# An encoder trunk on one core: three quarters of three turned inputs go through DRAM in 32x32 blocks

## The chip, the cores and the metric

The kernel runs on one core of a Trainium2 chip. The time is that of the whole program on the device, in microseconds (us); for the kernel before, the median of three runs is 2045.74 us (2043.22 to 2048.05).

A core has five engines that run their own instruction queues in order: TensorE (PE, with weight loads listed as PEld), VectorE (DVE), ScalarE (ACT), GpSimd (POOL) and SyncE (SP), which here issues most of the transfers. Semaphores tie the queues together.

## The reference

An encoder of two layers over 256 tokens of 2048 features, batch 1, float32. In each layer a token mixer of 12 heads and 4 cross-attention heads into 256 memory tokens work side by side on one input projection; their outputs are concatenated and go through one output projection; a squared-ReLU MLP of width 8192 follows. Layer 0 mixes by neighbourhood attention, layer 1 by grouped-query attention.

```python
m = rms_norm(mem, mem_norm)
h = x
for i in range(2):
    n = rms_norm(h, attn_norm[i])
    z = n @ w_in[i]                      # a_w_in in layer 0, b_w_in in layer 1
    ...                                  # mixer heads and memory heads
    h = h + concatenate([mix, cross]) @ w_o[i]
    n = rms_norm(h, mlp_norm[i])
    h = h + square(relu(n @ w_up[i])) @ w_down[i]
return rms_norm(h, final_norm)
```

where `rms_norm(x, g) = x * rsqrt(mean(x*x) + EPS) * g`. Since relu is homogeneous, `square(relu(c*x)) = c*c*square(relu(x))` for a positive factor c per token: an MLP may be fed with an input that is scaled by another positive factor than the exact one, if its output is corrected by the square of their ratio. The kernel uses this.

## The kernel before

**Precision.** Every float32 operand of a large product is split into a high part (rounded to the matmul's input type by ACT, `Copy`) and a low part (DVE, original minus high). A product is then three matmuls: high by high, low by high, high by low. So each weight chunk costs a load by SP, an ACT instruction and a DVE instruction (function `split`, lines 306 and 307) before PE uses it.

**Layout.** The running state `h` keeps tokens on partitions: 2 token tiles (`NT`) of 128, each 2048 features wide. A projection contracts over features, so its input must have features on partitions. It lies in a tile of one buffer, tag `wide` (`nT0`, `hT0`, `nT1`, `hT1` in turn): for each of 16 feature tiles k, 256 columns of the high part and 256 of the low part. Turning `h` into this form is what the change is about. In the kernel before `transposed` does it: for two feature tiles at a time, four PE transposes of 128x128 into one PSUM tile `pt_n` (line 324), then per feature tile `split_pair`: ACT multiplies by the gain and rounds (line 332), DVE computes the low part (line 333).

**Order of the work.** The program is a list of grains, run one after the other; a grain of a projection is 12 matmuls of 128x512 (or 24 of 128x256 in the up projection). `halves_of`, `up_grains`, `down_grains` and `plain_grains` make them. Loads and splits of a grain's weights are emitted some grains ahead (`ahead`, by default 8, 5 and 3 grains for its three stages; `SOON` 8, 5 and 4). After each grain `tick` counts one up and runs what `later(n, fn)` has put n ticks ahead. This gives every instruction its place in program order; a planner then simulates the engines and lets each engine take, at each simulated moment, the first instruction in program order that is ready. `past(fn)` adds an edge, so that what `fn` emits on ACT and DVE stands behind a given split in the queue of its engine.

**Buffers.** Weight halves of a projection have four buffers (`hi`, `lo` of pool `ring`); where a stage of the MLP is near, the halves `uh` and `ul` have two (pool `side`). Pool `side` also has the tags `U` (2 raw chunks), `b` (2, of 3 x 512 columns: pair chunks of the down projection) and `T` (2, of 4 x 512 columns: scaled blocks of `h`, later the fourth columns `t` of the pair chunks and raw chunks of the plain stage).

**Output projection and MLP input.** `add_o` computes the output projection in four blocks of 512 columns. Blocks 0 and 1 run interleaved (block 0 ends with its 14th grain, block 1 with its 16th), then block 2 (24th) and block 3 (32nd). `o_done` follows each block's last grain: it adds the block to `h` (line 687) and sums its squares (line 629). At block 2 `guard` estimates the mean square from three blocks (`GUARD`), POOL raises it to the power -1/2 (line 653), and `scaled` and `transposed` bring the three blocks to PE; block 3 is scaled beforehand in `begun`, gets its product added (line 704), and is turned at last. `inv` computes the ratio that corrects the MLP's output, from the exact mean square and the estimate `near`.

**From layer 0 to layer 1.** The last part of the down projection is the plain stage: four blocks of 512 columns, four grains each. `down_done` adds each block to `h` (line 880), sums its squares, and one tick later turns that block of `h` unscaled into `nT1`, on PE, for layer 1's input projection; that projection's results are scaled by `rstd` afterwards. Layer 1's projection starts with three chunks of the memory queries (`b_qm_done`), grains with `uh` and `ul`; chunk c reads the feature tiles of block c.

**A way through DRAM that is there already.** Layer 0's attention turns its 12 score tiles not on PE but by `turned`: DVE transposes every 32x32 block within its 32 partitions (line 393), and `moved` brings the blocks to their places: four SP transfers, one for each group of 32 partitions, write to a DRAM tile (line 358), and one POOL transfer reads it back (line 359).

Of the kernel before, what the change touches and what calls it, by code (L numbers as in the profile page):

```python
# [17 lines left out]
P = 128  # L18
# [18 lines left out]
PARTS = 8  # L37
PK = DFF // PARTS // P
STEPS = PK // 2
GUARD = 3  # L40

MOVING_AT = 160

# [35 lines left out]
def encoder_kernel(ctx: ExitStack, tc: tile.TileContext, t: dict, out: bass.AP):  # L79
# [70 lines left out]
    def halves_of(w):  # L150

        tiles = {}

        def load():
            tiles["raw"] = loaded(w.src, "U")

        def prep_early(hf):
            tiles[hf] = half_of_side(tiles["raw"], hf, MOVING_AT)

        def prep(hf):  # L160
            if hf == 0:
                tiles["raw"] = at.ring.tile([P, CH], F32, tag="raw", bufs=3, name="raw")
                nc.sync.dma_start(tiles["raw"], w.src)
            tiles[hf] = new_half(w.kind)
            split(*tiles[hf], tiles["raw"][:, hf * HALF : (hf + 1) * HALF])

        def run(hf):
            if hf == 0:
                w.start(w)
            hi, lo = tiles.pop(hf)  # L170
            if w.kind == "S":
                s_products(w, hf * (KT // 2), KT // 2, hi, lo)
            else:
                for i in range(NT):
                    m_products(w, w.first + 2 * hf, 2, i, hi, lo, w.begins and hf == 0, w.last and hf == 1)

        def after():
# [17 lines left out]
    def later(n, fn, *args):  # L195
        pending.append((state["tick"] + n, fn, args))
# [362 lines left out]
    def x_stats():  # L559
        ss = small.tile([P, NT], F32, tag="ss0", name="x_ss")  # L560
        for i in range(NT):
            for b in range(4):
                sq = at.work.tile([P, 512], F32, tag="b_y2", name="sq")
                nc.scalar.activation(sq, h[:, i, b * 512 : (b + 1) * 512], AF.Square, accum_out=ssq[0][:, i, b : b + 1])
        nc.vector.tensor_reduce(ss, ssq[0], axis=AX.X, op=ALU.add)
        box["x_col"] = keep.tile([P, NT], F32, name="x_col")
        nc.vector.tensor_copy(box["x_col"], rstd_of(ss, D, "x"))
        box["x_row"] = at.work.tile([P, SEQ], F32, tag="x_row", bufs=1, name="x_row")
        along_free(box["x_col"], box["x_row"])

# [69 lines left out]
    def past(fn, ins=None):  # L640

        a, v = ins or box["ready"]
        with tc.issue_after(a.ins), tc.issue_after(v.ins):
            fn()

    def o_done(layer, nb):
        which = 2 * layer

        def guard():

            box["near"] = mean_square(which, GUARD, "near")
            box["scale"] = keep.tile([P, NT], F32, tag="scale", name="scale")
            nc.gpsimd.tensor_tensor(box["scale"], box["near"], mhalf[:, :NT], op=ALU.pow)
            box["hT"] = wide(f"hT{layer}")

        def begun():

            y = at.side.tile([P, NT, 512], F32, tag="T", bufs=2, name="h_s")
            for i in range(NT):
                nc.scalar.activation(y[:, i, :], h[:, i, D - 512 :], AF.Copy, scale=box["scale"][:, i : i + 1])  # L660
            box["begun"] = y

        def scaled(b):
            y = at.side.tile([P, NT, 512], F32, tag="T", bufs=2, name="h_s")
            for i in range(NT):
                nc.scalar.activation(y[:, i, :], h[:, i, b * 512 : (b + 1) * 512], AF.Copy,
                                     scale=box["scale"][:, i : i + 1])
            transposed(box["hT"], lambda i, k: y[:, i, k % 4 * P : (k % 4 + 1) * P],
                       list(range(b * 4, b * 4 + 4)), (G_M0, G_M1)[layer])

        def inv():

# [7 lines left out]
        def f(w):  # L680
            if nb == 0:
                closed("work")
                at.side = opened("side", side="right")
            def add():
                for i in range(NT):
                    hs = h[:, i, nb * 512 : (nb + 1) * 512]
                    nc.vector.tensor_tensor(hs, w.ps[i], hs, op=ALU.add)

            def squares():
                for i in range(NT):  # L690
                    sum_squares(which, i, nb)

            if nb < 3:
                add()
                squares()
            if nb == GUARD - 1:
                later(1, guard)
                for b in range(GUARD):
                    later(2 + 2 * b, scaled, b)
                later(7, begun)  # L700
            if nb == 3:
                y = box["begun"]
                for i in range(NT):
                    nc.vector.scalar_tensor_tensor(y[:, i, :], w.ps[i], box["scale"][:, i : i + 1], y[:, i, :],
                                                   op0=ALU.mult, op1=ALU.add)
                box["ready"] = transposed(box["hT"], lambda i, k: y[:, i, k % 4 * P : (k % 4 + 1) * P],
                                          list(range(12, KT)), (G_M0, G_M1)[layer])
                later(4, past, add)
                later(6, past, squares)
                later(8, past, inv)  # L710
# [200 lines left out]
    def plain_grains(layer, nb):  # L911
# [9 lines left out]
        def prep(c, hf):  # L921
            if c == 0:
                own[c, hf] = half_of_side(own[0], hf, PLAIN_AT)
            else:
                own[c, hf] = tuple(at.mlp.tile([P, HALF], F32R, tag="bt"[hf] + x, name=f"{x}_p") for x in "hl")
                split(*own[c, hf], own[1][:, hf * HALF : (hf + 1) * HALF])

        PIECES = ((0, 0, 0, 2), (0, 1, 2, 2), (1, 0, 4, 2), (1, 1, 6, 2))

# [51 lines left out]
    def times_gf(nb):  # L981
        s = slice(nb * 512, (nb + 1) * 512)
        for i in range(NT):
            nc.vector.tensor_tensor(h[:, i, s], h[:, i, s], box["gf"][:, s], op=ALU.mult)

    def down_done(layer, nb):
        def f(w):
            for i in range(NT):
# [5 lines left out]
                return  # L994
            if nb == 0:
                box["nT"] = wide("nT1", 480)
            later(1, transposed, box["nT"], lambda i, k: h[:, i, k * P : (k + 1) * P],
                  list(range(nb * 4, nb * 4 + 4)), G_A1)
            if nb == 3:
                closed("mlp")  # L1000
                open_ring()

                def norm():
                    box["rstd"] = keep.tile([P, NT], F32, name="rstd1")
                    v = mean_square(1, 4, "full")
                    nc.gpsimd.tensor_tensor(box["rstd"], v, mhalf[:, :NT], op=ALU.pow)
                later(2, norm)
        return f

# [268 lines left out]
```

## Time and profile before

| | us |
|---|---|
| median of three runs | 2045.74 |
| lowest, highest | 2043.22, 2048.05 |
| the profiled execution | 2041.28 |
| its span, first to last instruction | 2039.5 |
| PE busy in it | 2018.9 |
| DVE busy | 1665.5 |
| ACT busy | 1241.9 |
| POOL busy | 125.3 |

The granted TensorE clock is full (mean 0.999). The busy time of PE is that of records that overlap: a matmul of 128x512 is recorded as about 390 ns, but one starts every 227 ns. So PE's own pace is read from starts, not from durations. The transfers move 440.16 MB, nearly all of it weights that SP loads.

### The profile page before, as it was taken

Reading aid. Unit: us, or ns where it says so; the run is one execution under the profiler, and the core shown is the slowest. Engines: PE = TensorE matmul, PEld = TensorE weight load, DVE = VectorE, ACT = ScalarE, POOL = GpSimd, SP = SyncE. Lnnn points to the kernel's source line nnn. Section 1 sums busy time; section 2 is a strip of 40 time slices with the busy share of each in tenths; the row PEclk is TensorE's granted clock in tenths of the full one; section 3 lists DMA queues with packets and bytes.
Section 4 is the critical chain, followed back from the end, with each engine's and each line's share of the span. In section 5 each row is a group of like instructions: output and inputs, shape, how many; then the busy total and the mean of one; then the engine's idle time right before and its main releaser. Section 6 shows DMA issues by size and latency. Waiting matters only on the chain.

```text
span 2039.5 us, 32742 instructions
## 1 busy us (share of the span) xinstructions
PE 2018.9 (99%) x13044; PEld 1827.2 (90%) x13044; DVE 1665.5 (82%) x2049; ACT 1241.9 (61%) x1628; POOL 125.3 (6%) x156
## 2 busy tenths in 40 slices
PE   8999999999999999999999999999999999999998
PEld 7899999889999999999988888889999999999986
DVE  6767677558989999989997667657999999999896
ACT  6655455456666666666656557556666666666654
POOL 0000000000000000010000001000000000000000
PEclk9999999999999999999999999999999999999999
DMA  7756666727778787777765454537777787777773
GB/s 281 276 200 202 218 211 213 287 83 239 231 220 240 222 239 229 224 236 232 229 207 220 176 170 145 199 113 235 236 230 231 222 239 228 231 224 230 230 220 137
DMA packets 101306, 440.16 MB, mean 216 GB/s; under 512 B 11424, under 2 KB 19232, under 8 KB 68000
## 3 DMA queue, kind: packets, MB, share of 16 engines
q1 hardware_dynamic: 82800, 402.40, 58.4%
q0 software_dynamic: 17776, 34.61, 9.1%
q8 instruction: 102, 1.67, 0.3%
q10 hardware_dynamic: 576, 1.05, 0.1%
q14 instruction: 52, 0.43, 0.1%
HBM read 401.32 MB, written 7.34 MB: 200 GB/s over the span
## 4 chain that ended last, share of the span: by engine, by line
PE 95%; DVE 2%; DMA 1%; issue 1%; ACT 1%; SPq 0%; POOLq 0%; POOL 0%; DVEq 0%; ACTq 0%
PE ps_u L742 11%; PE ps_u L740 11%; PE ps_u L741 11%; PE p L859 9%; PE p L858 9%; PE p L857 8%; PE ps_m L214 8%; PE ps_m L217 8%; PE ps_m L218 8%; PE ps_s L226 3%; PE ps_s L228 3%; PE ps_s L227 3%; DVE ul L307 1%; DMA raw<-in_w_km 1%; PE pt_n L324 1%
## 5 line engine op out<-in xcount | busy, mean ns | idle before, releaser
L742 PE MATMUL ps_u<-hT,ul 128*128 128x256 f32 x2048 | 567.1, 277 | 2.3 <-DVE ul L307 2.3
L740 PE MATMUL ps_u<-hT,uh 128*128 128x256 f32 x2048 | 565.6, 276 | 0.1
L741 PE MATMUL ps_u<-hT,uh 128*128 128x256 f32 x2048 | 565.6, 276 | 0.0
L306 ACT ACTIVATE uh<-raw_U 128x1024 fp32r<-128x1024 f32 x278 | 294.6, 1060 | 306.6 <-PE ps_u L741 280.2
L740 PEld LDWEIGHTS ps_u<-hT,uh 128*128 128x128 f32 x2048 | 384.5, 188 | 5.7 <-ACT uh L306 0.5
L741 PEld LDWEIGHTS ps_u<-hT,uh 128*128 128x128 f32 x2048 | 384.3, 188 | 5.4
L742 PEld LDWEIGHTS ps_u<-hT,ul 128*128 128x128 f32 x2048 | 384.4, 188 | 4.5 <-DVE ul L307 3.5
L307 DVE TENSOR_TENSOR lo<-raw,hi 128x1024 fp32r<-128x1024 f32 (+1 forms) x224 | 266.1, 1194 | 148.8 <-ACT hi L306 147.4
L307 DVE TENSOR_TENSOR ul<-raw_U,uh 128x1024 fp32r<-128x1024 f32 x278 | 337.2, 1218 | 38.9 <-ACT uh L306 38.8
L306 ACT ACTIVATE hi<-raw 128x1024 fp32r<-128x1024 f32 (+1 forms) x224 | 231.5, 1039 | 205.4 <-PE ps_m L218 112.2
L306 ACT ACTIVATE th<-t 128x2048 fp32r<-128x2048 f32 x112 | 215.1, 1921 | 124.4 <-PE p L859 116.1
L307 DVE TENSOR_TENSOR tl<-t,th 128x2048 fp32r<-128x2048 f32 x112 | 256.1, 2287 | 29.9 <-ACT th L306 29.4
L307 DVE TENSOR_TENSOR bl<-b,bh 128x1536 fp32r<-128x1536 f32 x112 | 196.0, 1750 | 0.3
L858 PE MATMUL p<-tl,a_s 128*128 128x512 f32 x448 | 176.1, 393 | 0.3 <-DVE tl L307 0.3
L859 PE MATMUL p<-th,a_s 128*128 128x512 f32 x448 | 176.3, 394 | 0.0
L306 ACT ACTIVATE bh<-b 128x1536 fp32r<-128x1536 f32 x112 | 166.2, 1484 | 7.7 <-PE p L859 1.3
L837 POOL DMA_DIRECT2D t<-b x112 | 96.4, 860 | 1157.1 <-DVE t L836 551.8
L857 PE MATMUL p<-th,a_s 128*128 128x512 f32 x448 | 163.6, 390 | 0.0
L859 PE MATMUL p<-bh,a_s 128*128 128x512 f32 x336 | 131.7, 392 | 0.0
L858 PE MATMUL p<-bl,a_s 128*128 128x512 f32 x336 | 131.0, 390 | 0.0
L228 PE MATMUL ps_s<-nT,lo 128*128 128x256 f32 x448 | 125.4, 280 | 0.0
L226 PE MATMUL ps_s<-nT,hi 128*128 128x256 f32 x448 | 125.2, 279 | 0.0
(237 smaller groups left out, 3770.2 us busy)
## 6 DMA issues: line engine op xcount, KB each, us to landing
raw_U<-in_w_up SPq DMA_DIRECT2D x128, 1024.0 KB, 6.4
b<-in_w_pair SPq DMA_DIRECT2D x112, 768.0 KB, 4.5
raw<-in_w_o SPq DMA_DIRECT2D x32, 1024.0 KB, 5.0
t<-in_w_pair SPq DMA_DIRECT2D x112, 256.0 KB, 3.4
t<-b POOLq DMA_DIRECT2D x112, 256.0 KB, 6.7
raw<-in_w_b SPq DMA_DIRECT2D x21, 1024.0 KB, 5.0
raw<-in_w_av SPq DMA_DIRECT2D x12, 1024.0 KB, 5.0
raw<-in_w_aq SPq DMA_DIRECT2D x12, 1024.0 KB, 4.9
```

The lines of the kernel that those rows point to most:

```text
L214: first = nc.tensor.matmul(w.ps[i], ah, hi[:, s], start=st, stop=False)
L217: nc.tensor.matmul(w.ps[i], ah, lo[:, s], start=False, stop=False)
L226: nc.tensor.matmul(ps, hi[:, s], acts[:, k, :SEQ], start=k == 0, stop=False)
L228: nc.tensor.matmul(ps, lo[:, s], acts[:, k, :SEQ], start=False, stop=k == KT - 1)
L306: first = nc.scalar.activation(dst_hi, src, AF.Copy)
L307: return first, nc.vector.tensor_tensor(dst_lo, src, dst_hi.bitcast(F32), op=ALU.subtract)
L740: nc.tensor.matmul(ps, hi[:, s], acts[:, k, :SEQ], start=k == 0, stop=False)
L741: nc.tensor.matmul(ps, hi[:, s], acts[:, k, SEQ:], start=False, stop=False)
L742: nc.tensor.matmul(ps, lo[:, s], acts[:, k, :SEQ], start=False, stop=k == KT - 1)
L857: nc.tensor.matmul(ps, a[:, 0, ai, :], hi[:, s], start=begins, stop=False)
L858: nc.tensor.matmul(ps, a[:, 0, ai, :], lo[:, s], start=False, stop=False)
L859: nc.tensor.matmul(ps, a[:, 1, ai, :], hi[:, s], start=False, stop=ends)
```

## The change

1. **The MLP input's factor.** Both MLPs' inputs are no longer scaled by the inverse root mean square of three finished blocks of `h`, but by that of the input of the same layer, which is known since before the projection: `x_col` in layer 0, `rstd` in layer 1. `inv` uses the corresponding mean squares (`x_mean`, `mean`). `guard` and `GUARD` are gone. So a block can be scaled as soon as it has been added.
2. **Blocks 0 to 2 of both MLP inputs** are scaled right after their add (`turning`), turned in 32x32 blocks by DVE and moved through DRAM (`turned_rows`). Block, room and read-back share one tile of tag `T`. `landed` makes the high and the low part from the read-back 6, 6 and 5 ticks later (`LANDED`), behind the last split emitted by then. Block 3 is left as it was.
3. **Blocks 0 to 2 of the second layer's input** go the same way, unscaled, through two tiles of tag `b` (`turned_input`), with `landed` 6 ticks later. Block 3 stays on PE.

`landed` emits per feature tile one ACT instruction over 256 columns and two DVE instructions over 128. `box["splits"]` now also collects the splits of `halves_of` and `plain_grains`, which `landed_past` needs.

```diff
-GUARD = 3
+TURNED = 3
+
+LANDED = 6, 6, 5
...
         box["x_col"] = keep.tile([P, NT], F32, name="x_col")
-        nc.vector.tensor_copy(box["x_col"], rstd_of(ss, D, "x"))
+        box["x_mean"] = keep.tile([P, NT], F32, name="x_mean")
+        nc.vector.tensor_scalar(box["x_mean"], ss, 1.0 / D, EPS, op0=ALU.mult, op1=ALU.add)
+        nc.gpsimd.tensor_tensor(box["x_col"], box["x_mean"], mhalf[:, :NT], op=ALU.pow)
...
+    def turned_rows(src, room, back):
+
+        nc.vector.transpose(room.rearrange("p (b k i j) -> p i k b j", b=4, k=4, i=2),
+                            src.rearrange("p i (k b r) -> p i k b r", k=4, b=4))
+        back = back.rearrange("p (a f) -> p a f", a=4)
+        moved(back, room.rearrange("p (b f) -> p b f", b=4))
+        return back
+
+    def landed(dst, back, b, which):
+
+        src = back.rearrange("p a (k i j) -> p k i a j", k=4, i=2)
+        for k in range(4):
+            n, g = b * 4 + k, gain(which, b * 4 + k)
+            hi, lo = (dst[:, n, x * SEQ : (x + 1) * SEQ].rearrange("p (i a j) -> p i a j", i=2, a=4) for x in range(2))
+            nc.scalar.activation(hi, src[:, k], AF.Copy, scale=g)
+            for i in range(NT):
+                nc.vector.scalar_tensor_tensor(lo[:, i], src[:, k, i], g, hi[:, i].bitcast(F32),
+                                               op0=ALU.mult, op1=ALU.subtract)
+
+    def landed_past(*args):
+        past(lambda: landed(*args), box["splits"][-1])
...
-        def guard():
-
-            box["near"] = mean_square(which, GUARD, "near")
-            box["scale"] = keep.tile([P, NT], F32, tag="scale", name="scale")
-            nc.gpsimd.tensor_tensor(box["scale"], box["near"], mhalf[:, :NT], op=ALU.pow)
+        def factors():
+
+            box["scale"] = box[("x_col", "rstd")[layer]]
+            box["near"] = box[("x_mean", "mean")[layer]]
             box["hT"] = wide(f"hT{layer}")
...
+        def turning():
+
+            y = at.side.tile([P, 2, NT, 512], F32, tag="T", bufs=2, name="h_s")
+            scaled(y[:, 0], nb)
+            x, room = (y[:, n].rearrange("p a b -> p (a b)") for n in range(2))
+            back = turned_rows(y[:, 0], room, x)
+            later(LANDED[nb], landed_past, box["hT"], back, nb, (G_M0, G_M1)[layer])
...
             if nb < 3:
                 add()
+                turning()
                 squares()
-            if nb == GUARD - 1:
-                later(1, guard)
-                for b in range(GUARD):
-                    later(2 + 2 * b, scaled, b)
-                later(7, begun)
+            if nb == 2:
+                later(3, begun)
...
+    def turned_input(nb):
+
+        x, y = (at.side.tile([P, 3 * 512], F32, tag="b", bufs=2, name=n)[:, : 2 * 512] for n in ("h_t", "h_b"))
+        back = turned_rows(h[:, :, nb * 512 : (nb + 1) * 512], x, y)
+        later(6, landed_past, box["nT"], back, nb, G_A1)
...
-            later(1, transposed, box["nT"], lambda i, k: h[:, i, k * P : (k + 1) * P],
-                  list(range(nb * 4, nb * 4 + 4)), G_A1)
+            if nb < TURNED:
+                later(1, turned_input, nb)
+            else:
+                later(1, transposed, box["nT"], lambda i, k: h[:, i, k * P : (k + 1) * P],
+                      list(range(nb * 4, nb * 4 + 4)), G_A1)
```

More of the change, by code (lines that the diff above doesn't have):

```diff
@@ L164, in prep @@
             tiles[hf] = new_half(w.kind)
-            split(*tiles[hf], tiles["raw"][:, hf * HALF : (hf + 1) * HALF])
+            box.setdefault("splits", []).append(split(*tiles[hf], tiles["raw"][:, hf * HALF : (hf + 1) * HALF]))
         def run(hf):
@@ L644, in past, with scaled @@
             fn()
+    def turned_rows(src, room, back):
[15 more added lines that the diff above has]
+        past(lambda: landed(*args), box["splits"][-1])
     def o_done(layer, nb):
         which = 2 * layer
-        def guard():
-            box["near"] = mean_square(which, GUARD, "near")
-            box["scale"] = keep.tile([P, NT], F32, tag="scale", name="scale")
-            nc.gpsimd.tensor_tensor(box["scale"], box["near"], mhalf[:, :NT], op=ALU.pow)
+        def factors():
+            box["scale"] = box[("x_col", "rstd")[layer]]
+            box["near"] = box[("x_mean", "mean")[layer]]
             box["hT"] = wide(f"hT{layer}")
[L656 to L664, printed above, removed]
+        def scaled(y, b):
             for i in range(NT):
@@ L667, in scaled, with begun @@
                                      scale=box["scale"][:, i : i + 1])
-            transposed(box["hT"], lambda i, k: y[:, i, k % 4 * P : (k % 4 + 1) * P],
-                       list(range(b * 4, b * 4 + 4)), (G_M0, G_M1)[layer])
+        def begun():
+            box["begun"] = at.side.tile([P, NT, 512], F32, tag="T", bufs=2, name="h_s")
+            scaled(box["begun"], 3)
+        def turning():
[4 more added lines that the diff above has]
+            later(LANDED[nb], landed_past, box["hT"], back, nb, (G_M0, G_M1)[layer])
         def inv():
@@ L683, in f @@
                 at.side = opened("side", side="right")
+                factors()
             def add():
@@ L925, in prep @@
                 own[c, hf] = tuple(at.mlp.tile([P, HALF], F32R, tag="bt"[hf] + x, name=f"{x}_p") for x in "hl")
-                split(*own[c, hf], own[1][:, hf * HALF : (hf + 1) * HALF])
+                box["splits"].append(split(*own[c, hf], own[1][:, hf * HALF : (hf + 1) * HALF]))
         PIECES = ((0, 0, 0, 2), (0, 1, 2, 2), (1, 0, 4, 2), (1, 1, 6, 2))
@@ L1004, in norm @@
                     box["rstd"] = keep.tile([P, NT], F32, name="rstd1")
-                    v = mean_square(1, 4, "full")
-                    nc.gpsimd.tensor_tensor(box["rstd"], v, mhalf[:, :NT], op=ALU.pow)
+                    box["mean"] = mean_square(1, 4, "mean")
+                    nc.gpsimd.tensor_tensor(box["rstd"], box["mean"], mhalf[:, :NT], op=ALU.pow)
                 later(2, norm)
```

## The prediction

> **What bounds the kernel now.** First the page's head and its busy times, then the busy time by stretch for the stretches that the change touches.
>
> ```profile
> span 2039.5 us, 32742 instructions
> PE 2018.9 (99%) x13044; PEld 1827.2 (90%) x13044; DVE 1665.5 (82%) x2049; ACT 1241.9 (61%) x1628; POOL 125.3 (6%) x156
> ```
> ```profile
> 386.00:402.00 16.00, 16.00 (x73) 13.24 (x72) 9.43 (x10) 9.04 (x14) 0.00 (x0) 1.00 0.87 341
> 420.00:438.00 18.00, 18.00 (x94) 15.21 (x93) 9.62 (x17) 9.98 (x19) 0.00 (x0) 1.00 0.06 16
> 1080.00:1095.00 15.00, 15.00 (x72) 12.44 (x71) 10.50 (x14) 8.56 (x14) 0.00 (x0) 1.00 0.37 131
> 1104.00:1120.00 16.00, 16.00 (x76) 13.23 (x75) 11.70 (x17) 10.81 (x16) 2.74 (x4) 1.00 1.02 398
> 1314.00:1330.00 16.00, 15.90 (x70) 12.81 (x70) 10.94 (x12) 10.86 (x17) 0.00 (x0) 1.00 1.00 407
> ```
>
> The columns after the stretch are its length, then busy time and count for PE, weight loads, DVE, ACT and POOL, then the granted clock, the DMA share and GB/s. PE is the bound in every one of them: full at a clock of 1.00, while DVE and ACT have a quarter to a half of their time free. So a matmul taken from PE shortens the program by its pitch on PE, as long as nothing that PE reads comes later. The third view is the chain that ended last, in order of time, at the places where PE turns the input (line 324), and the durations of those instructions.
>
> ```profile
> 422.77 1.53 PE pt_n L324 x14
> ...
> 432.71 0.87 PE pt_n L324 x8
> ...
> 1075.98 0.66 PE pt_n L324 x6
> 1087.80 0.66 PE pt_n L324 x6
> 1099.61 0.66 PE pt_n L324 x6
> ...
> 1142.33 0.66 PE pt_h L1062 x6
> ```
> ```profile
> L324 PE MATMUL pt_n<-ident,h_s x64: 270/272/273, 422.2 to 1367.8; 128*128 128x128 f32 x64
> ...
> L324 PE MATMUL pt_n<-ident,h x32: 270/272/273, 1075.1 to 1111.4; 128*128 128x128 f32 x32
> ```
>
> One grain, the unit of the work's order, is 12 matmuls of 128x512 in a projection; its length is the beat of the weight splits on ACT:
>
> ```profile
> 402.63 1.06 ACT L306 ACTIVATE hi<-raw 128x1024 fp32r<-128x1024 f32 x1 [1.66 <-PE ps_m L218]
> 405.35 1.06 ACT L306 ACTIVATE hi<-raw 128x1024 fp32r<-128x1024 f32 x1 [1.66 <-PE ps_m L218]
> ```
>
> 2.72 us. One transpose is recorded as 272 ns, but 14 of them pass in 1.53 us, 8 in 0.87 and 6 in 0.66: 0.109 us each on the path, since they overlap.
>
> **The change, part by part.**
>
> **Removed from PE.** Three of four 512-column blocks, at three places (both MLP inputs, the second layer's input): 9 blocks of 4 features by 2 token tiles, 72 of the 96 transposes. 72 x 0.109 = 7.9 us. The last block of each place stays on PE. Another angle: the blocks of the plain stage start 1087.80 - 1075.98 = 11.82 us apart, and four grains are 10.88, so eight transposes and what they disturb cost 0.94, and 72 of them 8.5. Bounds 7.9 and 8.5; I take 7.9, as the chain shows it directly at five places.
>
> In a sentence that the sum does without: the Trainium skill, "TensorE: Matmul & The Clock Gate", Part 4 (PE-mode transpose), gives about 275 ns for a transpose in a kernel's context; our 272 agrees, but priced so the change would save 72 x 0.275 = 19.8 us, as an estimate, and the chain's pitch of 0.109 says that this is latency, not occupancy.
>
> **Added to DVE and ACT.** The rows, then the price of a block:
>
> ```profile
> L333 DVE SCALAR_TENSOR_TENSOR hT<-pt_n,gains,hT 128x256 fp32r<-128x256 f32 x32 | 14.1, 479 | 10.0 <-ACT hT L332 9.7
> L332 ACT ACTIVATE hT<-pt_n,gains 128x256 fp32r<-128x256 f32 x32 | 13.8, 476 | 10.2 <-PE pt_n L324 8.1 <-DVE hT L333 1.9
> L393 DVE STREAM_TRANSPOSE sc_t<-sc 128x512 f32<-128x512 f32 x12 | 8.5, 708 | 0.2
> L666 ACT ACTIVATE h_s<-h,scale 128x512 f32<-128x512 f32 x12 | 7.8, 712 | 0.0
> L807 DVE TENSOR_TENSOR c<-c 128x128 f32<-128x128 f32 x224 | 58.9, 284 | 1.0
> L798 ACT ACTIVATE c<-c 128x256 f32<-128x256 f32 x128 | 53.5, 418 | 3.8
> L306 ACT ACTIVATE uh<-raw_U 128x1024 fp32r<-128x1024 f32 x278 | 294.6, 1060 | 306.6 <-PE ps_u L741 280.2 <-PE ps_m L218 15.4 <-DVE ul L307 3.3
> L307 DVE TENSOR_TENSOR ul<-raw_U,uh 128x1024 fp32r<-128x1024 f32 x278 | 337.2, 1218 | 38.9 <-ACT uh L306 38.8
> ```
>
> The 32x32 turn of 128x1024 isn't in the trace: between 1.22 (a 1024-wide DVE row) and 2 x 0.708 = 1.42; I take 1.3. The low half is now 8 DVE operations 128x128, not 4 of 128x256: 8 x 0.284 = 2.3 against 4 x 0.479 = 1.9. So DVE has 1.7 us more per block, 15 us over nine, in stretches where it is free for a third. ACT keeps 4 operations per block (0.42 to 0.48 each, as before) and its scaling, 2 x 0.71, which is moved: in the MLP inputs it no longer waits for three blocks' mean square but follows each block's add. On the path these are nothing, covered by PE's matmuls; what that cover is worth is in the stall terms below. The guard (two small DVE operations, a power on POOL) falls away, and x_mean takes the place of a copy: both hidden behind PE, nothing. Numbers for `inv` only change their source.
>
> **Added transfers.** Per block four SP writes of 128 KB and one POOL read of 512 KB: 36 and 9 in all, 9.4 MB on 440. The rows nearest:
>
> ```profile
> t<-b POOLq DMA_DIRECT2D x112, 256.0 KB, 6.7
> ...
> turn<-sc_t SPq DMA_DIRECT2D x48, 64.0 KB, 1.8
> sc<-turn POOLq DMA_DIRECT2D x12, 256.0 KB, 4.2
> ...
> km<-mem_k POOLq DMA_DIRECT2D x1, 1024.0 KB, 10.6
> vm<-mem_v POOLq DMA_DIRECT2D x2, 512.0 KB, 15.5
> ```
>
> The read's landing is bounded by 4.2 (half the size) and 15.5 (same size and queue, among 4 MB of weight loads); I take 6.5, near the smaller rows, because the traffic is mostly light where the blocks turn (share 0.37 at 1080 to 1095). From add to landing that is some 1.5 scaling, 1.3 turn, 2 issue, 2.5 write, 0.9 issue and 6.5 read: 14 to 15 us. By the Trainium skill, "DMA: Bandwidth & Descriptors", Anatomy of one DMA, a POOL transfer takes about 2.0 us plus bytes at 436 GB/s: an estimate of 3.2 for 512 KB; the 256 KB row's 4.2 against 2.6 by that rule says it is too short here, and by it the stalls below would be nil.
>
> **The new waits in the MLP inputs.** `landed` is due 5 grains after a block's end, 13.6 us, and stands in ACT's and DVE's queues ahead of later weight splits: if the read is late, those splits wait. Their cover: four buffers, so three grains, 8.2 us, less 1.06 + 1.22 and semaphores: 5.7 us. In layer 0 the expected lateness of about 1 us plus 4 x 0.48 of work fits. In layer 1 the start is worse:
>
> ```profile
> 1316.97 2.48 DVE L687 TENSOR_TENSOR h<-ps_m,h 128x512 f32<-128x512 f32 x4 [2.11 <-PE ps_m L218]
> ```
> ```profile
> 1311.94 0.33 SPq L163 DMA_DIRECT2D raw<-in_w_o  x1
> 1312.32 0.90 SPq L752 DMA_DIRECT2D raw_U<-in_w_up  x2
> 1314.01 0.81 SPq L822 DMA_DIRECT2D b<-in_w_pair  x2
> 1321.75 0.33 SPq L163 DMA_DIRECT2D raw<-in_w_o  x1
> ```
>
> Blocks 0 and 1 are added together, and 4.5 MB of loads issued from 1311.94 to 1314.8 take 11 us at 407 GB/s, to about 1323. Block 0's writes go out at about 1322, land near 1326, and the read lands between 1331.5 and 1334, due at 1331: ACT waits up to 3 us, then has two `landed` close together, 3 + 2 x 1.9 = 6.8 against 5.7. Stall 0 to 1.1; I take 0.4. SP waits for the turn with `raw<-in_w_o` behind it, about 1 to 2 us late; its split comes three grains on, so nothing. Blocks 0 and 1 are first read after block 3's products, 49 and 43 us after their ends (18 and 16 grains), block 2 nine grains, 24 us: not late.
>
> **The new waits at the second layer's input.** Here the last of the DVE adds of each block (line 880) sets the clock:
>
> ```profile
> 1071.40 1.40 DVE L880 SCALAR_TENSOR_TENSOR h<-ps_m,inv,h 128x512 f32<-128x512 f32 x2
> ...
> 1081.90 1.40 DVE L880 SCALAR_TENSOR_TENSOR h<-ps_m,inv,h 128x512 f32<-128x512 f32 x2
> ...
> 1093.71 1.40 DVE L880 SCALAR_TENSOR_TENSOR h<-ps_m,inv,h 128x512 f32<-128x512 f32 x2
> ```
> ```profile
> 1103.43 1.62 SPq L163 DMA_DIRECT2D raw<-in_w_b  x3
> ```
>
> Two buffers of tag b serve a whole block, so a block's read-back waits for the block before to be taken over by `landed`: a chain of 0.9 issue, 6.5 landing and about 3 for `landed`, 10.4 per block, on a beat of 4 grains, 10.9. It holds, barely. `landed` of block 2 comes behind the split that waits for the third grain of layer 1's first projection, about 19 us after block 2's end; its read starts some 9 us after that end and meets the three 1 MB loads of 1103.43. At 6.5 it lands at 16 to 17, at 10.6 at 20.5. PE needs it at 21.8. Then 4 ACT and 8 DVE operations, 2.3 us, stand among splits that have only two buffers there (2.72 less 1.06 + 1.22: 0.4 of cover). I take 0.3. POOL's `km` and `vm` reads queue behind that read and serve the memory attention, whose queries are turned at 1142, some 25 us later: nothing.
>
> **Sum:** -7.9 + 0.4 + 0.3 = -7.2. The profiled execution took 2041.28 for its span of 2039.5; it becomes 2034.1. It stood 4.5 below the median of the runs, 2045.74 (2043.22 to 2048.05); the median becomes 2038.5.
>
> **The rivals.**
>
> Half given back: the reads land late in the output projections. With 10.6 us in place of 6.5, layer 1's ACT waits 7 us: 7 + 1.9 - 5.7 = 3.2 on PE, and layer 0, with a share of 0.87 at 386 to 402, some 2. For it: ACT already waits on the turned scores; the row of the waits is below. Against: that wait never reached PE. -7.9 + 5.2 = -2.7: 2043.0.
>
> ```profile
> ACT pT L306 <- DMA sc<-turn: 10.9, 7, 3.3
> ```
>
> Slower: the two-buffer chain between the layers. If a read lands in 15.5, as vm's did, each link takes 0.9 + 15.5 + 3 = 19.4 on a beat of 10.9. Block 0's is over at 25 us, block 1's at 45, block 2's lands at 61 after block 0's end, 39.6 after its own; PE wanted it at 21.8: 18 us of stall, 2045.7 - 7.9 + 18 = 2056. It decides from links of about 13 us. For it: the vm row. Against: vm's reads were issued into a DMA share of 1.02, blocks 0 and 1 go into 0.37 to 0.56.
>
> More: the stalls at the start of the MLPs also shrink, about 1 us in each, 2036.5. Little speaks for it; their splits aren't touched.
>
> **How the numbers follow.** The forecast 0.55, half given back 0.25, slower 0.14, more 0.06. 0.2%, about 4 us, is what a measurement can tell from no change. Faster: 0.55 + 0.06 + a small part of the second: 0.65; within: 0.20; slower 0.15. The range goes from 2034.5 (the "more" case less half the spread of the runs) to 2047.0 (the whole gain given back, and 1.3 more); the likeliest alone has 2036 to 2041.
>
> **What would show it.** Line 324 with 24 matmuls; PE busy down by about 8; 9 turns on DVE near 1.3; 128 KB writes and 512 KB reads with their landing; ACT waits on the landing of h_s and h_b below 4 us and no PE gap over 1 us at 400 to 438, 1095 to 1125, 1320 to 1360. A PE wait on nT or hT, or on ACT's hi behind a DMA, would make it wrong.

## The result

| | before | after |
|---|---|---|
| median of six runs each, us | 2044.48 (2041.29 to 2050.87) | 2030.80 (2030.14 to 2036.89) |
| ratio, 95% interval | | 0.9937 (0.9921 to 0.9954) |
| the profiled execution, its span, us | 2041.28, 2039.5 | 2030.23, 2028.5 |

The kernel is faster by 13.7 us in this comparison. Two more comparisons of the same two kernels, each on a chip of its own, gave 0.9951 (0.9938 to 0.9963) and 0.9957 (0.9944 to 0.9969), 9.8 and 8.1 us by the medians. In the first of these two, one of the six executions of the kernel after took 5785.49 us; the ratio and the gain given here leave it out, and no trace shows what happened in it. The forecast was a gain of 7.2 and a time of 2038.5; the time lies below its range, which began at 2034.5.

### The profile page after: what moved, and what is told of

Same layout as the page of the kernel before. It is cut to its first block, busy times and chain, and to the rows that moved or that the text cites. A ratio compares the mean times of both kernels' runs of the same rounds, so it can differ in the third digit from the quotient of the medians.

```text
span 2028.5 us, 32745 instructions
## 1 busy us (share of the span) xinstructions
PE 2008.0 (99%) x12972; PEld 1818.2 (90%) x12972; DVE 1678.2 (83%) x2089; ACT 1243.0 (61%) x1628; POOL 130.7 (6%) x163
## 3 DMA queue, kind: packets, MB, share of 16 engines
q10 hardware_dynamic: 576, 1.05, 0.1%
## 4 chain that ended last, share of the span: by engine, by line
PE 96%; DVE 1%; DMA 1%; ACT 1%; issue 1%; SPq 0%; POOLq 0%; POOL 0%; ACTq 0%; DVEq 0%
PE ps_u L769 11%; PE ps_u L767 11%; PE ps_u L768 11%; PE p L886 9%; PE p L885 9%; PE p L884 9%; PE ps_m L216 8%; PE ps_m L219 8%; PE ps_m L220 8%; PE ps_s L228 3%; PE ps_s L230 3%; PE ps_s L229 3%; DMA raw<-in_w_km 1%; DVE ul L309 0%; PE pt_a L413 0%
## 5 line engine op out<-in xcount | busy, mean ns | idle before, releaser
L769 PE MATMUL ps_u<-hT,ul 128*128 128x256 f32 x2048 | 566.7, 277 | 2.1 <-DVE ul L309 2.1
L769 PEld LDWEIGHTS ps_u<-hT,ul 128*128 128x128 f32 x2048 | 384.4, 188 | 3.9 <-DVE ul L309 3.1
L229 PE MATMUL ps_s<-nT,hi 128*128 128x256 f32 x448 | 125.2, 280 | 0.0
L228 PE MATMUL ps_s<-nT,hi 128*128 128x256 f32 x448 | 125.2, 279 | 0.0
```

The costliest lines, as they stand in the source:

```text
L228: nc.tensor.matmul(ps, hi[:, s], acts[:, k, :SEQ], start=k == 0, stop=False)
L229: nc.tensor.matmul(ps, hi[:, s], acts[:, k, SEQ:], start=False, stop=False)
L769: nc.tensor.matmul(ps, lo[:, s], acts[:, k, :SEQ], start=False, stop=k == KT - 1)
```

## The profile after

The head of the page, its busy times and its transfers, as they were shown of before:

```profile
span 2028.5 us, 32745 instructions
...
PE 2008.0 (99%) x12972; PEld 1818.2 (90%) x12972; DVE 1678.2 (83%) x2089; ACT 1243.0 (61%) x1628; POOL 130.7 (6%) x163
...
DMA packets 107787, 449.59 MB, mean 222 GB/s; under 512 B 12145, under 2 KB 24561, under 8 KB 74481
```

PE lost 72 matmuls and 10.9 us of busy time, DVE gained 12.7, ACT 1.1, POOL 5.4, and 9.43 MB more were moved. PE is still the bound. Busy time by stretch, in the five stretches shown of before (columns as there), and the one in which layer 1's MLP input lands:

```profile
386.00:402.00 16.00, 16.00 (x72) 13.27 (x71) 10.83 (x11) 10.73 (x19) 0.55 (x1) 1.00 1.02 377
420.00:438.00 18.00, 18.00 (x97) 15.52 (x96) 7.35 (x14) 5.23 (x8) 0.54 (x1) 1.00 0.27 71
1080.00:1095.00 15.00, 15.00 (x68) 12.43 (x67) 13.31 (x23) 10.93 (x19) 0.56 (x1) 1.00 0.67 206
1104.00:1120.00 16.00, 16.00 (x75) 13.30 (x74) 14.40 (x22) 12.03 (x17) 0.10 (x1) 1.00 1.05 405
1314.00:1330.00 16.00, 16.00 (x72) 13.23 (x72) 12.59 (x11) 11.30 (x17) 1.15 (x2) 1.00 1.01 381
```
```profile
1330.00:1362.00 32.00, 32.00 (x174) 27.70 (x173) 20.52 (x41) 17.50 (x31) 0.53 (x1) 1.00 0.39 141
```

PE is full in all of them: no wait took the place of the transposes. Between the layers DVE has gone from 10.50 to 13.31 of 15 us, so little of its free time is left there. The chain that ended last, in order of time, in the plain stage:

```profile
1074.16 0.23 PE ps_m L216
1074.39 0.23 PE ps_m L219
...
1085.72 0.23 PE ps_m L216
...
1104.37 0.66 PE pt_n L326 x6
```

From 1074.16 to 1085.72 lie 11.56 us, 51 matmuls at an even pitch of 0.2267. Before, three groups of transposes stood in this stage, and the blocks started 11.82 apart where four even grains are 10.88. The six transposes at 1104.37 are those of block 3, which stays. The instructions on the tiles of the new way (duration ns min/median/max):

```profile
L666 DVE SCALAR_TENSOR_TENSOR hT<-h_s,gains,hT x48: 342/347/353, 409.3 to 1354.9; 128x128 fp32r<-128x128 f32 x48
...
L664 ACT ACTIVATE hT<-h_s,gains x24: 489/494/510, 408.0 to 1353.7; 128x256 fp32r<-128x256 f32 x24
...
L326 PE MATMUL pt_n<-ident,h_s x16: 272/272/273, 436.8 to 1358.8; 128*128 128x128 f32 x16
...
L652 DVE STREAM_TRANSPOSE h_s<-h_s x6: 1237/1240/1245, 388.2 to 1343.4; 128x1024 f32<-128x1024 f32 x6
```
```profile
L361 POOL DMA_DIRECT2D h_b<-turn x3: 540/556/562, 1078.3 to 1096.7; - x3
...
DMA to landing us min/median/max: 3.4/4.6/7.2
```

The last row belongs to the tile h_b, whose only transfers are the three reads of 512 KB. What PE and ACT waited for over the whole run (us in total, times, longest), from two views:

```profile
PE ps_s L228 <- ACT hi L308: 7.1, 1, 7.1
PE ps_u L769 <- DVE ul L309: 2.1, 4, 0.8
PE av L421 <- ACT pT L308: 1.0, 1, 1.0
PE ps_s L230 <- DVE lo L309: 0.8, 1, 0.8
PE ps_s L228 <- DVE km_s L350: 0.6, 1, 0.6
```
```profile
its engine sat idle before it (us, times) until:
...
  DMA h_s<-turn: 10.3, 2
```

None of PE's waits is on hT, nT or a split behind a landing. ACT did wait on landings, three times: 1.54 us for block 0 between the layers, and 3.66 and 6.69 us in the MLP inputs. No wait of PE came of it, and for the two longer ones the order of ACT's work shows why.

```profile
428.09 1.71 ACT L664 ACTIVATE hT<-h_s,gains 128x256 fp32r<-128x256 f32 x4 [3.66 <-DMA h_s<-turn]
...
1336.76 1.69 ACT L664 ACTIVATE hT<-h_s,gains 128x256 fp32r<-128x256 f32 x4
1338.51 1.06 ACT L308 ACTIVATE hi<-raw 128x1024 fp32r<-128x1024 f32 x1
1339.48 1.69 ACT L664 ACTIVATE hT<-h_s,gains 128x256 fp32r<-128x256 f32 x4
...
1352.51 1.71 ACT L664 ACTIVATE hT<-h_s,gains 128x256 fp32r<-128x256 f32 x4 [6.69 <-DMA h_s<-turn]
1357.55 1.06 ACT L308 ACTIVATE uh<-raw_U 128x1024 fp32r<-128x1024 f32 x1 [3.32 <-PE ps_u L768]
```

Both marked waits on `h_s` are those of block 2, the last that is read, and the split behind the longer one waited another 3.32 us for PE itself (behind the other, 7.20). Layer 1's blocks 0 and 1, for which the prediction priced a stall, found their data there and had a split between them.

**Where the time went.** The starts of the same PE matmul in two traces, subtracted, show where the traces part. Each column is a profile against the first profile of before; a stretch's number is what it became longer (us; stretches with less than 0.3 in every column are left out):

| stretch | after | after, 2nd | after, 3rd | before, 2nd |
|---|---|---|---|---|
| start to 61 | -0.21 | +0.02 | +0.22 | -0.51 |
| 61 to 82, products of the memory keys | -0.83 | -0.83 | -0.83 | -0.83 |
| 400 to 452, layer 0's MLP input | -2.77 | -2.77 | -2.68 | 0.00 |
| 452 to 500, start of the MLP | -0.09 | -0.07 | +0.85 | -0.06 |
| 500 to 1030, the MLP | 0.00 | +0.94 | 0.00 | 0.00 |
| 1062 to 1130, between the layers | -2.80 | -2.80 | -2.80 | -0.01 |
| 1330 to 1380, layer 1's MLP input | -2.85 | -2.85 | -2.86 | +0.01 |
| 1930 to 1975, late in layer 1's MLP | -1.23 | -1.23 | -1.23 | -1.23 |
| all to the last matmul | -10.78 | -9.66 | -8.88 | -2.53 |

The three places of the change give 8.4 us in all three profiles, to a tenth. The rest is in stretches that the change doesn't touch, and a second profile of the kernel before differs from the first there by as much.

## The experiments

**Is the rest scatter? Both kernels again.** No edit: the kernel before, and the kernel after twice, on two chips.

> The kernel before, unchanged, once more. The two profiles in hand differ by 11.0 us in span, of which 8.5 lie at the three turned inputs, 1.2 at waits on late fourth columns of the pair chunks near 1941 and 1968 us, and 0.8 in the memory keys' products at 61 to 80 us, where nothing was changed. Theory 1 (scatter): these two last parts, and the spread of the runs before from 2041 to 2051, differ from execution to execution; this profile shows them at other places or sizes, and the ratio is 1.000 within 0.2%. Theory 2 (the change makes them): this profile shows the same 1.2 and 0.8 us at the same places.

> The changed kernel, unchanged, once more. Theory 1 (PE's own time: 72 transposes at 0.118 us each, 8.5 us, and the rest scatter between executions): ratio 0.9958, some 8.5 us. Theory 2 (the change is worth the whole 13 us): ratio 0.9937 again.

> The changed kernel once more, beside the next two on one chip. Theory 1 (PE's own time, the rest of the first comparison scatter): ratio 0.9958, 8.5 us. Theory 2 (13 us): ratio 0.9937.

The kernel before against its own other runs: 1.0001 (0.9991 to 1.0011), median 2041.37. The kernel after: 2031.34 (without the execution of 5785 us) and 2032.11, with the ratios given above. Busy time by stretch, of the first profile of before and then of the second:

```profile
60.00:80.00 20.00, 20.00 (x171) 19.91 (x170) 15.02 (x28) 13.67 (x26) 0.00 (x0) 1.00 1.00 394
1925.00:1970.00 45.00, 44.56 (x296) 40.03 (x295) 42.78 (x45) 27.81 (x28) 3.43 (x4) 1.00 0.68 207
```
```profile
60.00:80.00 20.00, 20.00 (x170) 19.69 (x170) 15.35 (x28) 13.64 (x27) 0.00 (x0) 1.00 0.99 395
1925.00:1970.00 45.00, 45.00 (x308) 41.34 (x308) 44.22 (x46) 28.39 (x28) 3.45 (x4) 1.00 0.67 210
```

With the kernel unchanged, PE is full at 1925 to 1970 in the one and not in the other. So 0.83 + 1.23 = 2.06 us of the first difference between the traces can come and go without the change; whether the change makes the 1.23 rarer is taken up below. The first comparison's 13.7 has a before whose median, 2044.48, is 3 to 4 us above those of the later four (2041.12, 2041.55, 2040.18, 2041.54).

**One place at a time.** The kernel after with `TURNED = 0`, so that the second layer's input stays on PE; and the kernel before with only that input moved.

```diff
-TURNED = 3
+TURNED = 0
```

> The change without its part between the layers: the second layer's input is turned wholly on PE again. Theory 1 (PE's own time, 0.118 us for each of 48 transposes): 5.7 us less than before. Theory 2 (the new factor or the earlier scaling brings the surplus): 10 us or more less than before.

> The kernel before with the part between the layers alone: three of four blocks of the second layer's input go through DRAM, and the MLP inputs stay on PE with their factor from three blocks. Theory 1 (PE's own time, 24 transposes): 2.8 us less. Rival (two buffers in a chain of reads, late at the end): 0, or slower.

Measured 0.9967 (0.9955 to 0.9979), 5.9 us by the medians, and 0.9979 (0.9970 to 0.9988), 4.3 us. In the traces the three places moved by -2.76, 0 and -2.85 in the first and by 0, -2.80 and 0 in the second. So the terms are separate, and none depends on the others.

**The new factor without the way through DRAM.** Both MLP inputs are scaled early, by the layer input's factor, and are turned on PE as before, as many ticks later as `landed` would be due; `TURNED = 0`.

```diff
-            y = at.side.tile([P, 2, NT, 512], F32, tag="T", bufs=2, name="h_s")
-            scaled(y[:, 0], nb)
...
-            later(LANDED[nb], landed_past, box["hT"], back, nb, (G_M0, G_M1)[layer])
+            y = at.side.tile([P, NT, 512], F32, tag="T", bufs=2, name="h_s")
+            scaled(y, nb)
+            later(LANDED[nb], transposed, box["hT"], lambda i, k: y[:, i, k % 4 * P : (k % 4 + 1) * P],
+                  list(range(nb * 4, nb * 4 + 4)), (G_M0, G_M1)[layer])
```

> The change with all turning left on PE: the MLP inputs have the factor of the layer input and each block is scaled right after its add, then turned on PE 5 grains later; the second layer's input is turned on PE. Theory 1 (only the transposes count): ratio 1.000 within 0.1%. Rival (the guard and its mean square of three blocks held something up): 1 us or more under the kernel before, ratio 0.9995 or less.

Measured 1.0000 (0.9991 to 1.0009). Without the guard and its power on POOL and with the early scaling alone, nothing is gained that can be told from none (the interval is 1.8 us either way); the gain is that of the transposes.

**The turn and the transfers taken out.** `turned_rows` gives its source back at once, and `landed` reads the block as it is. The turn, the writes and the reads are left out, so the MLPs and layer 1 work on wrongly placed numbers; the instructions of `landed` stay.

```diff
-        nc.vector.transpose(room.rearrange("p (b k i j) -> p i k b j", b=4, k=4, i=2),
-                            src.rearrange("p i (k b r) -> p i k b r", k=4, b=4))
-        back = back.rearrange("p (a f) -> p a f", a=4)
-        moved(back, room.rearrange("p (b f) -> p b f", b=4))
-        return back
+        return src
...
-        src = back.rearrange("p a (k i j) -> p k i a j", k=4, i=2)
+        src = back.rearrange("p i (k a j) -> p k i a j", k=4, a=4)
```

> The changed kernel without the 32x32 turn, the writes and the reads: the high and low parts are made straight from the unturned block, so the output is not the reference's; PE's matmuls, ACT's and DVE's other work and their places stay. Theory 1 (the way through DRAM is hidden whole, the gain is PE's 72 transposes at 0.118 us): the same as the changed kernel, 8.5 us under the kernel before, ratio 0.9958 within 0.1%. Rival (the 9.4 MB and the reads in the queue cost something on the path): 1 us or more below the changed kernel, ratio 0.9953 or less.

Measured 0.9958 (0.9946 to 0.9971); the places moved by -2.49, -2.80 and -2.57, no more than with the transfers. So the way through DRAM is hidden, and 8.4 us is all that the removal of these transposes can give in this order of the work.

**How much cover is left: each block read twice.** POOL reads every block a second time to the same place, so a block arrives one more issue and landing later.

```diff
         nc.gpsimd.dma_start(dst, x)
+        for _ in range(again):
+            nc.gpsimd.dma_start(dst, x)
...
-        moved(back, room.rearrange("p (b f) -> p b f", b=4))
+        moved(back, room.rearrange("p (b f) -> p b f", b=4), 1)
```

> The changed kernel with each of the nine blocks read back from DRAM twice, one read after the other, into the same place: the landing comes later by one issue and one landing, 5 to 7 us. Theory 1 with cover to spare (the reads have more room than this): the same as the changed kernel, ratio 0.9958. Rival (the cover is nearly used, as the prediction had it: 5.7 us less the work itself): 2 to 6 us slower than the changed kernel, ratio 0.997 to 0.999.

Measured 0.9969 (0.9958 to 0.9981), 6.6 us by the medians where the kernel after has 8 to 10. In the trace the first place keeps its gain (-2.55), between the layers 1.4 are left of 2.9, and layer 1's MLP input keeps 0.14: 4.3 lost. The last block's two reads between the layers, by POOL's timeline, were issued 8.9 us apart:

```profile
1103.35 0.54 POOL L361 DMA_DIRECT2D h_b<-turn  x1 [6.23 <-DMA turn<-h_t]
...
1112.29 0.58 POOL L363 DMA_DIRECT2D h_b<-turn  x1 [5.25 <-DMA h_b<-turn]
```

The view of PE's waits has four that the kernel after lacks (this kernel's helper is two lines longer, so its L771 is L769 there):

```profile
PE ps_m L219 <- DVE ul L309: 0.5, 1, 0.5
PE ps_m L216 <- ACT nT L666: 0.5, 1, 0.5
PE ps_u L769 <- ACT uh L308: 0.4, 1, 0.4
PE ps_u L770 <- DVE hT L668: 0.3, 1, 0.3
```

The mechanism of the "half given back" rival is real: what one more issue and landing takes, 5 to 9 us between the layers, two of the three places can't cover. In the kernel after it doesn't set in.

**The transposes priced by doubling.** The kernel before, each of the 72 transposes done twice in a row into the same place.

```diff
+            for _ in range(times):
+                for b, k in enumerate(ks[a : a + 2]):
+                    for i in range(NT):
+                        nc.tensor.transpose(pt[:, b, i * P : (i + 1) * P], src(i, k), ident)
...
+                       list(range(b * 4, b * 4 + 4)), (G_M0, G_M1)[layer], 2)
...
+                  list(range(nb * 4, nb * 4 + 4)), G_A1, 2 if nb < 3 else 1)
```

> The kernel before with its 72 transposes of the first three blocks done twice, the second time onto the same result, so PE's price of one is measured without any transfer. Priced by the step from block to block (0.118 us): 8.5 us slower, ratio 1.0042. By the spacing inside a run of transposes (0.109): 7.9 us, 1.0038. By the recorded duration (0.272): 19.6 us, 1.0096. The trace's starts at the three places tell the first two apart.

Measured 1.0080 (1.0066 to 1.0094), some 16 us: twice what was expected. At the three places the trace grew by 2.62, 2.59 and 2.79, 8.0 together, 0.111 for each added transpose; its chain has them at the prediction's pitch:

```profile
421.99 3.17 PE pt_n L325 x29
...
430.62 1.75 PE pt_n L325 x16
```

3.17 / 29 and 1.75 / 16 are both 0.109. The other 7 to 8 us arose elsewhere, in the MLPs' pair grains (those of the down projection whose weights come in pair chunks): 3.8 before 1030, 0.7 before 1062 and 3.9 before 1930. From 960 to 1050 the kernel before and then this one, busy time by stretch, each with the row of DVE's groups for the fourth columns (busy, mean ns, idle before and what ended it):

```profile
960.00:1050.00 90.00, 90.00 (x608) 82.34 (x606) 84.72 (x85) 56.24 (x58) 6.91 (x8) 1.00 0.75 225
```
```profile
L836 DVE TENSOR_TENSOR t<-t,b 128x512 f32<-128x512 f32 x8 | 5.5, 686 | 1.8 <-DMA t<-in_w_pair 1.7
```
```profile
960.00:1050.00 90.00, 87.79 (x582) 78.92 (x581) 80.80 (x85) 55.91 (x56) 7.40 (x9) 1.00 0.71 212
```
```profile
L837 DVE TENSOR_TENSOR t<-t,b 128x512 f32<-128x512 f32 x9 | 6.2, 689 | 10.1 <-DMA t<-in_w_pair 8.3 <-issue 1.8
```

Here DVE is busy 94% of the time in the kernel before, and PE lives off its `tl`, the low part of the fourth columns `t`. With 8.3 us of DVE's time lost to `t` loads that came late, PE lost 2.2. So the experiment confirms the pitch, and its total is not a price of transposes. Why these loads came late in it was not settled.

**Does the late loss belong to the change?** By then no profile of a kernel with layer 1's MLP input moved had the late loss of 1.23 us, and four of five with that input on PE had it, two of them in part. Two more profiles of the kernel before, and the two MLP inputs one at a time (in the other layer the blocks are turned on PE, as in the experiment on the factor; `TURNED = 0`):

```diff
+            if layer == 0:
+                y = at.side.tile([P, NT, 512], F32, tag="T", bufs=2, name="h_s")
+                scaled(y, nb)
+                later(LANDED[nb], transposed, box["hT"], lambda i, k: y[:, i, k % 4 * P : (k % 4 + 1) * P],
+                      list(range(nb * 4, nb * 4 + 4)), G_M0)
+                return
```

> The kernel before, unchanged, one more profile of it. So far the stretch from 1930 to 1975 us, late in the second MLP, where DVE is busy for 95 to 100% of the time, is 1.23 us longer in the first profile of the kernel before, and in none of nine profiles of kernels that move the second MLP's input through DRAM; one other profile of the kernel before does not have it either. Theory A, that the loss comes with the order of the kernel before: this profile has it (TensorE busy about 44.6 of 45 us from 1925 to 1970). Theory B, scatter between executions of any kernel: it has it or not, and says nothing by itself.

> The kernel before again, a further profile for the same question: by theory A the late stretch is again about 1.2 us longer than after the change, by theory B it may be either; two more profiles without it would leave theory A with one of four.

> Only the second MLP's input goes through DRAM; the first MLP has the new factor but stays on TensorE, as does the second layer's input. The term of its 24 transposes is 2.8 us. Theory A: 2.8 and the 1.2 of the late stretch, 4.0 in all, a ratio of 0.9980. Theory B: 2.8, a ratio of 0.9986, and the profile has the late loss or not.

> Only the first MLP's input goes through DRAM; the second MLP has the new factor but is turned on TensorE. Theory A and theory B: 2.8 us from 24 transposes, a ratio of 0.9986; by theory A the profile keeps the late loss of 1.2 us, by theory B it has it or not.

Theory A as it stood, that the loss comes with the order of the kernel before, falls: both profiles of the kernel before are without most or all of it (-0.95 and -1.23 in the stretch 1930 to 1975). They lost elsewhere: the first 1.75 before 1030 and 2.01 before 1930, the second 4.37 from 1420 to 1930. But the two variants went as theory A said: layer 0 alone has the loss (PE busy 44.41 of the 45 us from 1925 to 1970), and layer 1 alone has lost most of it (-0.88). Over all profiles it shows whole in three of eight with layer 1's MLP input on PE and in part (0.8 and 0.5) in two more, while ten with that input moved have at most 0.35 of it, so a weaker form, that the change makes it rarer, stays open. Busy time from 1420 to 1930 in the first profile of before, and then in this last one, with a row of its view of PE's waits:

```profile
1420.00:1930.00 510.00, 510.00 (x3435) 466.81 (x3434) 468.57 (x504) 332.74 (x333) 41.97 (x49) 1.00 0.77 230
```
```profile
1420.00:1930.00 510.00, 507.71 (x3396) 462.74 (x3396) 465.11 (x501) 328.64 (x331) 41.97 (x49) 1.00 0.76 229
```
```profile
PE p L858 <- DVE tl L307: 2.0, 2, 1.3
```

It is the same program: the pair grains lose 0 to 4.4 us in one execution or another, at places that differ. Layer 1 alone gave 0.9981 (0.9971 to 0.9990), layer 0 alone 0.9974 (0.9965 to 0.9983); in the traces -2.85 and -2.77 at their places, as their terms say. Layer 0 alone is faster than its term: 4.7 us by the medians, and 2.8 is outside its interval (3.5 to 7.1). Taken with `between_alone` the three single steps sum to 12.0 by the medians, the whole change to 8.1 to 9.8 on the later chips. A part of each difference may be that the kernel before loses more in the pair grains than its variants mostly do. The lowest runs of all show the two floors: 2038.75 before and 2030.14 after, 8.6 apart, which is near the three terms; the medians of before stand 1.4 to 2.8 above that floor on the later chips, those of after 1.2 to 2.0. Whether the change makes such losses rarer can't be told from these runs.

**A step further.** Block 3 between the layers goes through DRAM too (`TURNED = 4`), twice measured; and, on top of it, the score tiles of layer 0's four memory heads go through DRAM as those of its mixer heads do (`blocks` gives the ticks of their three steps), 16 transposes fewer on PE.

```diff
-TURNED = 3
+TURNED = 4
...
-            attention([(q, box["km"][:, hd, :], None, head_of(box["vm"], hd), NH + hd, box["cat"])], 1)
+            attention([(q, box["km"][:, hd, :], None, head_of(box["vm"], hd), NH + hd, box["cat"])], 1, blocks=(0, 4, 5))
```

> The changed kernel with all four blocks of the second layer's input through DRAM: 8 transposes fewer on PE. Theory 1 (0.118 us each, and the last block is read only after three chunks of the next projection, so its landing is in time): 0.94 us under the changed kernel, ratio 0.9954. Rival (the fourth block lands after PE wants it): slower than the changed kernel by the lateness, 1 to 5 us.

> The kernel with all four blocks of the second layer's input through DRAM, again: 0.9 us under the changed kernel by theory 1, ratio 0.9954.

> As the run before, and the score tiles of layer 0's four memory heads go through DRAM as those of its twelve mixer heads do: 16 PE transposes fewer. Theory 1: 16 x 0.118 = 1.9 us less, ratio 0.9945. Rival (the heads' outputs or a buffer of scores come too late): slower than the run before.

The fourth block: 0.9946 (0.9933 to 0.9958), median 2029.97, the lowest of all, and 0.9957 (0.9943 to 0.9970), 2031.41. From 1062 to 1215 the traces have 3.54 and 3.58 us in place of 2.89, a gain of some 0.65 over the kernel after; in the time it can't be told from none. The memory heads' way through DRAM makes it slower than that, 0.9970 (0.9959 to 0.9981), although PE has 16 transposes less: the product with the values, `av`, waits a second time, beside the 1.0 us that the kernel after has too,

```profile
126.93 0.39 PE L216 MATMUL ps_m<-hi,nT 128*128 128x512 f32 x1
129.43 0.39 PE L421 MATMUL av<-pT,vm 128*128 128x256 f32 x1 [2.12 <-ACT pT L308]
```

and the trace is 2.6 longer from 82 to 400 than the kernel after's. The wait is most of that; the rest was not followed up.

## Why the prediction was right, and where it was wrong

**What bounds the kernel.** Right: PE is full at a clock of 1.00, and a matmul that is taken away shortens the program by about its pitch.

**The term of the transposes.** It failed in size: -7.9, from 0.109 each, where the three places gave 8.4 to 8.5, 0.117 to 0.118 for each transpose removed. The 0.109 is right for a transpose inside a group, as the doubling shows (0.109 in the chain, 0.111 in the sum). The switch from and to the products is only a small part of what it leaves out. By the starts in the trace of before, from the last product in front of a group to the second one behind it and less the products' own pitch, the groups with their edges cost 2.65, 2.71 and 2.65 us at the three places: 8.0, or 0.111 each. The other 0.4 lies among the products around, 0.1 between the layers and 0.1 and 0.2 at the MLP inputs, there in part in the first products of the up projection. The prediction had a number near the total in hand as its "other angle" (0.94 per block, 8.5 in all) and chose the lower bound because the chain showed it "directly at five places". The chain showed the inside of the groups; the block's beat showed the program. That the beat of the plain stage also fits the MLP inputs is in part luck, as the groups there cost 0.88 per block.

**The stall in layer 1's MLP input (+0.4).** It did not come, but the step that priced it was wrong in two terms that cancelled, which is luck. The prediction let a block take 14 to 15 us from its add to its landing, and had `landed` due 13.6 us after the block's end. The adds of blocks 0 and 1, and the transfers issued from 1314 to 1335 with their median landing:

```profile
1310.23 2.48 DVE L716 TENSOR_TENSOR h<-ps_m,h 128x512 f32<-128x512 f32 x4 [2.11 <-PE ps_m L220]
```
```profile
turn<-h_s SPq DMA_DIRECT2D x8, 128.0 KB, 7.6
...
h_s<-turn POOLq DMA_DIRECT2D x2, 512.0 KB, 8.6
```

The adds end at 1312.71. The writes landed after 7.6 us where 2.5 was taken, the reads after 8.6 where 6.5 was taken, so block 0 landed at 1334.17, 21.5 us after the adds. But its `landed` stands at 1336.76, 24.1 us after them, nearly nine grains and not five; block 1's, at 1339.48, had its data since 1337.74. The room left was 2.6 and 1.7 us. ACT's wait moved to block 2, 6.69 us, above the prediction's bound of 4 us for such waits, and the split behind it had 3.32 us to spare.

**The two-buffer chain between the layers, and the +0.3.** The chain was wrong as a step, not only in its size. It let block 1's read wait until `landed` had taken over block 0. The reads' issues on POOL, and block 0's `landed` on DVE, say otherwise:

```profile
1078.33 0.56 POOL L361 DMA_DIRECT2D h_b<-turn  x1 [38.05 <-DVE h L907]
1085.39 0.56 POOL L361 DMA_DIRECT2D h_b<-turn  x1 [6.49 <-DMA turn<-h_t]
1096.66 0.54 POOL L361 DMA_DIRECT2D h_b<-turn  x1 [10.72 <-DMA turn<-h_t]
```
```profile
1083.46 2.19 DVE L666 SCALAR_TENSOR_TENSOR nT<-h_b,gains,nT 128x128 fp32r<-128x128 f32 x8 [0.82 <-ACT nT L664]
```

Blocks 1 and 2 waited for their own writes, and block 1's read went out at 1085.39, before DVE was done with block 0 at 1085.65. By the addresses of the built kernel, block 0 is turned into one buffer and read back into the other; block 1 is turned into the first and read back into that same one, whose content has already been written out; block 2 uses the second for both. Two of the three reads were faster than the 6.5 us taken, 4.6 and 3.4, and block 2's took 7.2. The +0.3 stood for block 2's `landed` among splits with 0.4 us of cover: no wait of PE came of it, and why the cover was enough was not worked out. By the rule of the Trainium skill, "DMA: Bandwidth & Descriptors", Anatomy of one DMA, the estimate for 512 KB is 3.2 us. Three of the nine reads, 3.4 to 3.5, come near it, and the other six took 4.6 to 8.7; its consequence, no stall, is what happened, in layer 1 for another reason.

**Durations.** 1.24 us for the turn against 1.3 taken. `landed` is recorded as 494 ns on ACT against 0.48 and 347 ns on DVE against 284, but its instructions overlap: eight on DVE pass in 2.19 us where 2.3 was taken. DVE's sum was below the 15 taken, 12.7. All of it lay under PE's matmuls, as said.

**From the sum to the median.** The sum was made against the profiled execution, 2041.28, and gave 2034.1 for it; then the prediction added the 4.5 by which the median of three runs stood above it. That failed most: later medians of before are 2040.2 to 2041.6, so the profiled execution was the typical one and the three runs were high; whether by chance or by their chip isn't known. Of the 7.7 between 2038.5 and the median 2030.8, 4.5 are this step, 0.5 to 0.6 the transposes, 0.7 the stalls that did not come; the last 2 are of the size of the two losses (0.83 and 1.23) that the first profile of before had and its second did not.

**The rivals.** "Half given back": its condition came in part, as four of the six reads of the MLP inputs took 7.5 to 8.7 us, but nothing was given back, since `landed` stood later than priced; the loss appears once the blocks come some 5 us later still. "Slower": its chain does not exist in that form, and no read between the layers took over 7.2 (its 39.6 us should be 39.2, 61 less two beats of 10.9; nothing hangs on it). "More", from shorter stalls where the MLPs start: near nothing, the waits of `ps_u` on `ul` are 2.1 us after and 2.3 before.

## What to carry to other kernels

On an engine that is full, price what you remove by the beat of the stage with and without it, not by the pitch inside a group: here the beat came to 8.5, the pitch to 7.9, and the places gave 8.4. Make the sum against a profiled execution, and before adding a median's distance ask whether three runs place it: here they stood 4 us too high, more than half of the effect. And find out whose writes a buffer waits for before you build a chain on it: which of two tiles takes which buffer decided a rival here.

## What the runs showed that was not expected

- The same 256-wide products of the memory keys ran at a start-to-start pitch of 117 to 118 ns from 61 to 82 us in two profiles (the first of before and that of the factor alone) and at 113 in all others, worth 0.83 us, with the same code and a granted clock of 1.00. The 256-wide products of the up projections have the same two pitches: the third profile of after has 118 from 455 to 479, which is its +0.85 in the table, and the third further one of before, `before_third_look`, from 1376 to 1408, where the first has 113. What sets it is open.
- Where DVE is at 92 to 95% and feeds PE, executions of one program differ by up to 4.4 us in 500, at places that change, and a change elsewhere (the doubled transposes) can add 7 to 8 us there.
- The way through DRAM, 36 writes and 9 reads, cost PE nothing that the traces show, at a DMA share from 0.27 to 1.05 in the stretches shown.
